# One set of buffer pools through the whole kernel, and output stages that take all first block products before the second ones

## The chip, the cores and the metric

The kernel runs on one core of one Trainium2 chip. A core has a matrix engine (TensorE, PE in the profile; its weight loads are PEld), a vector engine (VectorE, DVE), an activation engine (ScalarE, ACT), a general engine (GpSimd, POOL), a queue engine (SyncE, SP) and 16 DMA engines. Each engine runs its own instruction stream in order. Memory on the chip is SBUF (working tiles, 128 partitions) and PSUM (eight banks, which TensorE writes). The metric is the device time of one execution in microseconds (us).

## What is computed

A decoder block on `x` (1024 tokens by 1024 channels), all in float32:

```python
h = rms_norm(x, norm_g)
z = h @ w_in                      # 1024 x 9216: q_r k_r v_r gate_r q_d k_d v_d gate_d mg_r mg_d
o_r = rms_norm(retention(q_r, k_r, v_r)) * silu(gate_r)      # branch 0
o_d = rms_norm(diff_attention(q_d, k_d, v_d)) * silu(gate_d) # branch 1
m = sigmoid(mg_r) * (o_r @ ret_w_o) + sigmoid(mg_d) * (o_d @ diff_w_o)
out = x + m @ w_out
```

## The kernel before

A float32 operand of a matrix product is cut into a high and a low part (`split`, `cut`: ScalarE rounds the high part, VectorE subtracts it), and a product takes three matmuls: high by high, high by low, low by high.

**Mixer part.** Two retention groups (`rqk`, `rv`) and eight attention heads (`d0` to `d7`) project their columns of `w_in` with the normalised, transposed input `hT`. Weight tiles come from the pool `wpool` (tag `w`, `NWS` = 11 buffers; raw loads with tag `wraw`, 3 buffers). The small pieces of each token block are put on a clock of ticks (`after`, `among`) and dealt out between the projection's matmuls. The pool `dp` holds the attention heads' tiles.

**Output part.** The gates' columns of `w_in` (16 pairs of 128-wide strips, numbered `q`), the two branch projections (`y0`, `y1`) and the final projection (`out`) are products of a 2 by 2 block matrix with a 2 by 2 block matrix, done in Winograd's form with seven block products. A block product is 12 matmuls of 128x512 (`product`: four chunks of the contraction, three matmuls each). The right-hand side is `r11`, `r21`, `r22` and the combinations `t1` to `t4`, each in one home tile (`HOME`), so a stage's `t2` can only be written when the stage before has read its own for the last time. `early_r` loads and cuts `r11` and `r21`; `late_r` loads the blocks, forms the sums on VectorE and cuts them (for the gates it takes them from `hT`). Loads and sums pass through staging tiles with tag `rs` (6 buffers). The left-hand side of a pair: the first two block products (`firsts`; the bank is called `X`, with operands `la`) give the block c(0,0) and a partial result `p1`; the other five are in `Pair.one` (banks `y`, `w`, `z`, against `t2`, `t3`, `t1`) and `Pair.two` (`w` against `t4`, `z` against `r22`). `rest_ops` loads a pair's strips (`ra`, `rb`; tag `raw`, 3 buffers), forms four sums on VectorE (tag `sf`, 4 buffers) and cuts five operands (tag `l`, 8 buffers). `rests` interleaves `two` of one pair with `one` of the next, and prepares the pair after.

**Which tiles meet.** `first_duo(q)` computes the first two block products of two gate pairs in the mixer part, for q = 0 to 10; `first[q]` in DRAM keeps them. Pairs 12 to 15 are done at the start of the output part by `firsts("hm", ...)`. Between the two parts `mixers.close()` gives up `wpool`, `gp` (result tiles `ft`, tag `gt`) and the PSUM pool `ps`; the output part opens `act2`, `lp`, `fp` and a PSUM pool `pb` of eight banks over the same memory and over that of `dp`.

**Merging the branches.** Each branch block is multiplied by its gate (`sg`, loaded into tag `ld`, 2 buffers) and goes to `md` in DRAM: branch 0 by a plain store from SP, branch 1 by a DMA from GpSimd that adds to what is there (line 919). The final projection reads its left-hand side from `md`; the rows of `md[0]` come from branch pairs 0 and 1, those of `md[1]` from pairs 2 and 3.

**Order.** The program is traced in the order of the code, and a planner (`schedule_with_timeline_sim`) turns it into one static instruction stream for each engine, from a model of times and with program order as priority. A tile with a tag gets a buffer when an earlier tile of that tag is released.

## Time and profile before

| | |
|---|---|
| median of three runs | 1324.86 us (1323.21 to 1325.03) |
| profiled execution | 1322.55 us, of which 1320.8 us span |
| TensorE | busy 1264.3 us, 96% of the span |
| VectorE | busy 950.9 us, 72% |
| ScalarE | busy 651.4 us, 49% |
| GpSimd | busy 265.4 us, 20% |
| mixer part, without its last drain | up to 792 us |
| gate pairs | about 800 to 1065 us |
| branch projections | about 1062 to 1228 us |
| final projection | about 1218 us to the end |

TensorE is busy nearly throughout, so time is lost where it stands still or where its granted clock is below full speed. The shares of the other engines are averages over parts that differ much, and are read by stretch.

### The profile page before, as it was taken

To read this page: it belongs to the slowest core of one execution; us is meant where nothing else is said; L and a number is where in the kernel's file an instruction comes from. 1 tells how busy PE (TensorE), PEld (TensorE's weight loads), DVE (VectorE), ACT (ScalarE), POOL (GpSimd) and SP (SyncE) were. 2 spreads that over 40 slices of the span, in tenths; PEclk is the share of its full clock that TensorE was granted. 3 is DMA by queue.
4 is the path that set the end of the run, shared out by engine and by line. 5 is a ranking of instruction groups with operands and counts; after the bars stand their busy time and mean duration, and the time that the engine had idled before them with its cause. 6 is when DMAs were issued, how large, how long until landed. Compare 5 with 4: busy or idle time off the path is not lost.

```text
span 1320.8 us, 19793 instructions
## 1 busy us (share of the span) xinstructions
PE 1264.3 (96%) x6836; PEld 1113.4 (84%) x6836; DVE 950.9 (72%) x2016; ACT 651.4 (49%) x1448; POOL 265.4 (20%) x371
## 2 busy tenths in 40 slices
PE   7999999999999999999999997899989999998698
PEld 5888888889999999999999885687778888876586
DVE  7436435737786877777687838987876699998884
ACT  6235123527575766767676724434454454442420
POOL 3134113323333534243333100000000000012000
PEclk9999999999999999999999998899999999999799
DMA  7202120431010101102020326578876578998963
GB/s 259 66 29 72 57 72 8 125 107 49 9 57 9 57 10 56 55 11 65 9 72 9 120 89 201 189 256 276 298 251 208 160 245 274 301 277 178 253 191 112
DMA packets 157750, 169.95 MB, mean 129 GB/s; under 512 B 9921, under 2 KB 108369, under 8 KB 157649
## 3 DMA queue, kind: packets, MB, share of 16 engines
q1 hardware_dynamic: 154816, 163.68, 38.4%
q0 software_dynamic: 2832, 5.00, 2.6%
q8 instruction: 54, 0.88, 0.3%
q14 instruction: 48, 0.39, 0.1%
HBM read 122.51 MB, written 46.14 MB: 128 GB/s over the span
## 4 chain that ended last, share of the span: by engine, by line
PE 67%; DVE 13%; DMA 11%; issue 4%; ACT 3%; POOL 2%; SPq 1%; DVEq 0%; ACTq 0%; POOLq 0%
PE z_d L121 18%; PE z_rv L121 7%; PE z_rqk L121 6%; PE fb L130 5%; PE sps L533 5%; PE dops L573 5%; PE z_h L130 3%; PE w_h L130 3%; PE aT L560 2%; DMA og<-c_h 2%; PE X_out L130 2%; PE z_out L130 2%; PE w_out L130 2%; PE y_h L130 1%; DMA r_o<-og 1%
## 5 line engine op out<-in xcount | busy, mean ns | idle before, releaser
L121 PE MATMUL z_d<-w_d,hT 128*128 128x384 f32 x1536 | 303.5, 340 | 1.4 <-DVE nsq L488 1.4
L121 PEld LDWEIGHTS z_d<-w_d,hT 128*128 128x128 f32 x1536 | 264.3, 188 | 4.5 <-ACT V L479 1.7
L539 ACT ACTIVATE S<-S,ast 128x256 f32<-128x256 f32 (+7 forms) x128 | 99.0, 774 | 33.4 <-DVE ast L535 32.0
L533 PE MATMUL sps<-K,Q 128*128 128x512 f32 (+5 forms) x384 | 107.5, 363 | 0.5 <-ACT Q L516 0.5
L919 POOL DMA_DIRECT2D md<-c_y x16 | 13.9, 869 | 435.0 <-DVE ls_y L663 372.7
L121 PE MATMUL z_rv<-w_rv,hT 128*128 128x512 f32 x384 | 98.8, 397 | 0.0
L121 PE MATMUL z_rqk<-w_rqk,hT 128*128 128x512 f32 x384 | 94.1, 398 | 0.9 <-ACT hT L283 0.9
L121 PEld LDWEIGHTS z_rqk<-w_rqk,hT 128*128 128x128 f32 x384 | 70.9, 190 | 15.8 <-ACT hT L283 1.6
L573 PE MATMUL dops<-V,aTs 128*128 128x128 f32 x576 | 78.7, 275 | 0.0
L121 PEld LDWEIGHTS z_rv<-w_rv,hT 128*128 128x128 f32 x384 | 68.7, 188 | 11.8
L573 PEld LDWEIGHTS dops<-V,aTs 128*128 128x128 f32 x576 | 76.6, 191 | 2.2 <-ACT aTs L562 0.2
L535 DVE CUSTOM_DVE_ANT_0 S<-sps,ndist 128x512 f32<-128x512 f32 (+5 forms) x128 | 67.9, 533 | 10.4 <-PE sps L533 10.1
L130 PE MATMUL fb<-hT,fw 128*128 128x512 f32 x288 | 71.5, 396 | 0.0
L91 POOL TENSOR_TENSOR nss<-ms_n,mh 128x4 f32<-128x4 f32 x64 | 67.2, 1051 | 4.3
L533 PEld LDWEIGHTS sps<-K,Q 128*128 128x128 f32 x384 | 63.2, 189 | 3.1 <-ACT Q L516 1.5
L130 PEld LDWEIGHTS fb<-hT,fw 128*128 128x128 f32 x288 | 52.7, 188 | 10.2
L490 POOL TENSOR_TENSOR nsq<-nsq,gh 128x256 f32<-128x256 f32 x64 | 47.5, 746 | 63.7 <-DVE nsq L488 62.4
L550 DVE SCALAR_TENSOR_TENSOR S<-S,ast,S 128x128 f32<-128x128 f32 (+3 forms) x64 | 55.5, 868 | 1.2
L130 PE MATMUL z_h<-hT,ls_h 128*128 128x512 f32 x192 | 48.4, 401 | 6.0 <-DVE c_h L810 5.9
L130 PE MATMUL y_h<-t_h,ls_h 128*128 128x512 f32 x192 | 49.0, 398 | 3.3 <-ACT t_h L662 3.3
L662 ACT ACTIVATE ls_h<-s_h 128x512 fp32r<-128x512 f32 x64 | 38.6, 621 | 27.0 <-PE z_h L130 18.6
L130 PE MATMUL w_h<-t_h,l_h 128*128 128x512 f32 x192 | 48.4, 398 | 3.5 <-DVE u_h L822 3.5
(251 smaller groups left out, 2760.3 us busy)
## 6 DMA issues: line engine op xcount, KB each, us to landing
wr_d<-in_w_in_dram SPq DMA_DIRECT2D x96, 128.0 KB, 2.8
ra_h<-in_w_in_dram SPq DMA_DIRECT2D x16, 512.0 KB, 4.2
rb_h<-in_w_in_dram SPq DMA_DIRECT2D x16, 512.0 KB, 5.3
s<-sg SPq DMA_DIRECT2D x32, 256.0 KB, 4.2
fr<-in_w_in_dram SPq DMA_DIRECT2D x12, 512.0 KB, 4.8
first<-ft SPq DMA_DIRECT2D x24, 256.0 KB, 2.0
og<-c_h SPq DMA_DIRECT2D x24, 256.0 KB, 4.4
sg<-c_h SPq DMA_DIRECT2D x24, 256.0 KB, 3.3
```

The lines of the kernel that those rows point to most:

```text
L91: nc.gpsimd.tensor_tensor(out_t, ms, mh[:, :n], ALU.pow)
L121: nc.tensor.matmul(o, a[k][:, i0, asl], b[k][:, i1, bsl], start=(k == 0 and j == 0), stop=(k == NK - 1 and j == 2))
L130: nc.tensor.matmul(bank, L[:, i0, j * P:(j + 1) * P], R[:, j, i1, :], start=(start and j == 0 and i == 0), stop=(j == 3 and i == 2), skip_ ...
L490: nc.gpsimd.tensor_tensor(sq, sq, hd["g"], ALU.mult)
L533: nc.tensor.matmul(sp[:, :m], hd["Q"][t][:, j, e, :], hd["K"][:, j, c], start=(e == 0), stop=(e == 1))
L535: nc.vector.tensor_tensor_reduce(sb[:, c], sp[:, :m], ndist[:, S - n + m * f:S - n + m * f + m], -slope, FMAX if f == 0 else st[:, j:j + 1 ...
L539: nc.scalar.activation(sb[:, :n], sb[:, :n], AF.Exp, bias=st[:, j:j + 1], scale=-1.0, accum_out=st[:, 2 + j:3 + j])
L550: nc.vector.scalar_tensor_tensor(S0[:, :n], S1[:, :n], st[:, 6:7], S0[:, :n], ALU.mult, ALU.add)
L560: nc.tensor.transpose(tp[:, b * P:(b + 1) * P], A[:, c:c + P], ident)
L573: nc.tensor.matmul(o[:, :P], aT[:, b, :], hd["V"][f][:, b, :], start=(kb == 0), stop=(kb == t))
L662: nc.scalar.activation(dst_hi, src, AF.Copy)
L919: nc.gpsimd.dma_start(m, t, accum_op=ALU.add)
```

## The change

`wpool`, `gp` and `ps` stay open to the end (`mixers` is gone) with `NWS` = 10. The output part uses their tiles: cut operands take tag `w` (10 buffers, before `l` with 8), raw strips tag `wraw` (3, as `raw` had), results tag `gt` (3, as `c` had), and the eight banks are the tags `pj`, `s`, `tr`, `o` of `ps` in a fixed turn. The four sums of `rest_ops` have lost their own tag and share `rs`, which now has 7 buffers for both. Pairs 12 to 15 go through `first_duo` as the others do, behind `late_r("h", None)` in the code; the weights of pairs 12 and 13 are asked for in `first_duo(10)`. `firsts` takes the first block product of all four pairs, then the second of all four. The last pair of branch 1 (p = 3, four blocks) loads its part of `md`, adds on VectorE and stores it from SP.

```diff
-NWS = 11
+NWS = 10
...
-    mixers = ExitStack()
-    wpool = mixers.enter_context(tc.tile_pool(name="wpool", bufs=NWS))
-    ps = mixers.enter_context(tc.tile_pool(name="ps", bufs=2, space=bass.MemoryType.PSUM))
+    wpool = ctx.enter_context(tc.tile_pool(name="wpool", bufs=NWS))
+    gp = ctx.enter_context(tc.tile_pool(name="gp", bufs=3))
+    ps = ctx.enter_context(tc.tile_pool(name="ps", bufs=2, space=bass.MemoryType.PSUM))
...
         for q in range(4, 12, 2):
-            first_duo(q, (lambda q=q: more(q + 2, q + 3)) if q < 10 else (lambda: None))
+            first_duo(q, lambda q=q: more(q + 2, q + 3))
         drain()
-    mixers.close()
...
-    pb = ctx.enter_context(tc.tile_pool(name="pb", bufs=8, space=bass.MemoryType.PSUM))
...
     def stage(name):
-        return lpool.tile([P, 512], F32, tag="rs", name=name, bufs=6)
+        return lpool.tile([P, 512], F32, tag="rs", name=name, bufs=7)
...
     def left(name, src):
-        L = lpool.tile([P, 2, 512], F32R, tag="l", name=name, bufs=8)
+        L = wpool.tile([P, 2, 512], F32R, tag="w", name=name)
...
     def raw_l(name):
-        return lpool.tile([P, 4, 2, P], F32, tag="raw", name=name, bufs=3)
+        r = wpool.tile([P, 2, 512], F32, tag="wraw", name=name, bufs=3)
+        return r.rearrange("p a (b n) -> p (a b) n", n=P).rearrange("p (j s) n -> p j s n", s=2)
...
     def rest_ops(name, src):
...
-        s1, s2, s3, s4 = (lpool.tile([P, 4, P], F32, tag="sf", name=f"s{i}_{name}", bufs=4)
+        s1, s2, s3, s4 = (stage(f"s{i}_{name}").rearrange("p (j n) -> p j n", n=P)
                           for i in range(1, 5))
...
+    turn = [0]
+
     def bank(name):
-        return pb.tile([P, 512], F32, tag="b", name=name)
+        tag, n = (("pj", NPJ), ("s", NS), ("tr", NTR), ("tr", NTR),
+                  ("pj", NPJ), ("s", NS), ("tr", NTR), ("o", 1))[turn[0] % 8]
+        turn[0] += 1
+        return pst(tag, name, n)
...
     def firsts(name, srcs, done):
...
+        ops = [load(0, i) for i in range(2)]
+        for kh in range(2):
+            for i in range(n):
+                k = kh * n + i + 2
+                if k < 2 * n:
+                    ops.append(load(k // n, k % n))
+                run(product(X[i], ops[kh * n + i], RB["r21" if kh else "r11"], kh == 0))
+                if kh == 0:
+                    p1.append(temp("p1", f"p1_{name}{i}", 4))
+                    nc.scalar.activation(p1[i], X[i], AF.Copy)
+                else:
+                    done(i, X[i])
         return p1
...
-    p1 = firsts("hm", [hsrc(q) for q in range(12, 16)], keep(12))
     late_r("h", None)
-    for i, t in enumerate(p1):
-        nc.sync.dma_start(first[12 + i][:, 0, :], t)
-    rests([gate_pair(q) for q in range(16)])
+    first_duo(12, lambda: more(14, 15))
+    pairs = [gate_pair(q) for q in range(16)]
+    first_duo(14, pairs[0].prep)
+    rests(pairs, True)
...
                 m = rows(md[i // 4][:, i % 4], half)
-                if br == 0:
+                if p == 3 and br == 1:
+                    o = temp("ld", f"m{i}{half}", 2)
+                    nc.sync.dma_start(o, m)
+                    nc.vector.tensor_tensor(t, t, o, ALU.add)
+                if br == 0 or p == 3:
                     nc.sync.dma_start(m, t)
                 else:
                     nc.gpsimd.dma_start(m, t, accum_op=ALU.add)
```

## Rows read from the trace of the kernel before

**Rows 1.** The page: busy time, share of span and instructions of each engine.

```profile
PE 1264.3 (96%) x6836; PEld 1113.4 (84%) x6836; DVE 950.9 (72%) x2016; ACT 651.4 (49%) x1448; POOL 265.4 (20%) x371
```

**Rows 2.** Stretches: length, then busy us (instructions) by engine, clock, DMA share, GB/s.

```profile
300.00:740.00 440.00, 438.83 (x2906) 426.49 (x2905) 334.48 (x975) 307.67 (x821) 161.96 (x237) 1.00 0.14 40
760.00:792.00 32.00, 32.00 (x172) 27.27 (x170) 10.04 (x21) 8.55 (x16) 2.25 (x3) 1.00 0.24 90
792.00:860.00 68.00, 52.87 (x203) 41.30 (x202) 61.41 (x102) 27.41 (x48) 0.00 (x0) 0.87 0.61 192
860.00:1060.00 200.00, 192.80 (x838) 157.81 (x837) 151.59 (x242) 88.26 (x145) 0.00 (x0) 0.99 0.73 241
1060.00:1165.00 105.00, 105.00 (x465) 86.91 (x465) 101.45 (x170) 50.04 (x88) 2.17 (x3) 1.00 0.84 274
1206.00:1240.00 34.00, 18.92 (x76) 14.90 (x75) 24.25 (x40) 10.12 (x18) 6.05 (x7) 0.82 0.96 232
1240.00:1250.00 10.00, 9.99 (x35) 7.55 (x34) 10.00 (x18) 6.11 (x11) 0.00 (x0) 0.77 1.08 339
```

**Rows 3.** Timeline of TensorE between the two parts: start us, us, instructions, idle before.

```profile
789.34 2.99 PE L130 MATMUL fb<-hT,fw 128*128 128x512 f32 x12
800.34 1.22 PE L130 MATMUL X_hm<-hT,la_hm 128*128 128x512 f32 x2 [8.02 <-ACT la_hm L662]
803.05 3.35 PE L130 MATMUL X_hm<-hT,la_hm 128*128 128x512 f32 x7 [1.48 <-ACT la_hm L662]
```

**Rows 4.** The chain that ended last, between the two parts: start us, us, what.

```profile
790.34 2.27 DMA ot_d<-doT
...
793.16 3.19 DMA first<-ft
...
797.39 4.96 DMA ra_hm<-in_w_in_dram
```

**Rows 5.** Timeline of ScalarE and GpSimd where `dp` opens over a closed pool.

```profile
286.15 0.39 ACT L478 ACTIVATE nsq<-z_d 128x256 f32<-128x256 f32 x1 [6.03 <-DMA ot_r<-roTs]
...
286.30 0.29 POOL L469 COPY gh<-gains 128x128 f32<-128x128 f32 x1 [9.62 <-DMA ot_r<-roTs]
```

**Rows 6.** Timeline of VectorE: the first instruction of `late_r("h", None)`.

```profile
796.62 0.69 DVE L670 TENSOR_TENSOR r11s_h<-hT 128x512 f32<-128x512 f32 x1 [3.51 <-DMA o<-ot_r]
```

**Rows 7.** Timeline of TensorE between branch 1 and the final projection.

```profile
1217.87 1.22 PE L130 MATMUL X_out<-r_w,la_out 128*128 128x512 f32 x2 [3.42 <-ACT la_out L662]
1218.89 3.79 PE L130 MATMUL w_y<-t_o,l_y 128*128 128x512 f32 x12
1222.52 2.43 PE L130 MATMUL X_out<-r_w,la_out 128*128 128x512 f32 x10
1224.79 2.88 PE L130 MATMUL z_y<-r_o,ls_y 128*128 128x512 f32 x12
1239.34 2.88 PE L130 MATMUL X_out<-r_w,la_out 128*128 128x512 f32 x5 [11.66 <-ACT la_out L662]
```

**Rows 8.** The chain that ended last, into that second stop of TensorE.

```profile
1227.46 6.86 DMA md<-c_y
...
1234.38 4.20 DMA ra_out<-md
...
1238.65 0.64 ACT la_out L662
```

**Rows 9.** DMA issues: queue, count, size, median us from issue to landing.

```profile
s<-sg SPq DMA_DIRECT2D x32, 256.0 KB, 4.2
...
md<-c_y SPq DMA_DIRECT2D x16, 256.0 KB, 3.7
md<-c_y POOLq DMA_DIRECT2D x16, 256.0 KB, 5.7
```

**Rows 10.** Timeline of SP: last strip load of the gates, first of branch 0.

```profile
1015.54 0.38 SPq L762 DMA_DIRECT2D rb_h<-in_w_in_dram  x1
...
1027.04 2.12 SPq L753 DMA_DIRECT2D ra_y<-in_ret_w_o_dram  x4
```

More of the change, by code (lines that the diff above doesn't have):

```diff
@@ L248, in proj @@
         return z
-    gp = mixers.enter_context(tc.tile_pool(name="gp", bufs=3))
     with tc.tile_pool(name="rq", bufs=8) as rq, ExitStack() as early:
@@ L744, in raw_l @@
     def raw_l(name):
-        return lpool.tile([P, 4, 2, P], F32, tag="raw", name=name, bufs=3)
-    def first_ops(name, src):
-        L = []
-        for kh in range(2):
-            if kh == 0:
-                r = raw_l(f"ra_{name}")
-            nc.sync.dma_start(r[:, :, kh:kh + 1, :], src(kh, 0, 1))
-        for kh in range(2):
-            L.append(left(f"la{kh}_{name}", r[:, :, kh, :]))
-        return L
+        r = wpool.tile([P, 2, 512], F32, tag="wraw", name=name, bufs=3)
+        return r.rearrange("p a (b n) -> p (a b) n", n=P).rearrange("p (j s) n -> p j s n", s=2)
     def rest_ops(name, src):
@@ L773, in rest_ops, with load @@
         return A, [left(f"l22_{name}", l22), left(f"ls4_{name}", s4)]
+    turn = [0]
     def bank(name):
-        return pb.tile([P, 512], F32, tag="b", name=name)
+        tag, n = (("pj", NPJ), ("s", NS), ("tr", NTR), ("tr", NTR),
+                  ("pj", NPJ), ("s", NS), ("tr", NTR), ("o", 1))[turn[0] % 8]
+        turn[0] += 1
+        return pst(tag, name, n)
     def temp(tag, name, bufs=None):
+        if tag == "c":
+            return gp.tile([P, 512], F32, tag="gt", name=name, bufs=3)
         return fp.tile([P, 512], F32, tag=tag, name=name, **(dict(bufs=bufs) if bufs else {}))
     def firsts(name, srcs, done):
-        ops = [first_ops(f"{name}{i}", s) for i, s in enumerate(srcs[:2])]
-        X, p1 = [], []
-        for i in range(len(srcs)):
-            X.append(bank(f"X_{name}{i}"))
-            run(product(X[i], ops[i][0], RB["r11"], True))
-            p1.append(temp("p1", f"p1_{name}{i}", 4))
-            nc.scalar.activation(p1[i], X[i], AF.Copy)
-            if i > 0:
-                run(product(X[i - 1], ops[i - 1][1], RB["r21"], False))
-                done(i - 1, X[i - 1])
-                if i + 1 < len(srcs):
-                    ops.append(first_ops(f"{name}{i + 1}", srcs[i + 1]))
-        run(product(X[-1], ops[-1][1], RB["r21"], False))
-        done(len(srcs) - 1, X[-1])
+        n = len(srcs)
+        X = [bank(f"X_{name}{i}") for i in range(n)]
+        p1 = []
+        def load(kh, i):
+            r = wpool.tile([P, 2, 512], F32, tag="wraw", name=f"rf_{name}{kh}{i}", bufs=3)
+            r = r[:, 0, :].rearrange("p (j n) -> p j n", n=P)
+            nc.sync.dma_start(r.unsqueeze(2), srcs[i](kh, 0, 1))
+            return left(f"la{kh}_{name}{i}", r)
+        ops = [load(0, i) for i in range(2)]
[10 more added lines that the diff above has]
+                    done(i, X[i])
         return p1
@@ L831, in two, with rests @@
             self.c(0, 1, self.z, self.u2, ALU.subtract)
-    def rests(pairs):
-        pairs[0].prep()
+    def rests(pairs, ready=False):
+        if not ready:
+            pairs[0].prep()
         before = iter(())
@@ L854, in hsrc @@
         return strips(w_in, pair_col[q])
-    def keep(q):
-        def done(i, b):
-            t = temp("c", f"c11_{q + i}")
-            nc.vector.tensor_copy(t, b)
-            nc.sync.dma_start(first[q + i][:, 1, :], t)
-        return done
     def gate_pair(q):
```

## Prediction, made before the changed kernel was run

> **What bounds the kernel now.** I read the page's engine line first, then stretches, then the timelines and the chain of waits at the places where TensorE stops. TensorE is busy 96% of the span [rows 1], so the question is where the rest goes. By stretches [rows 2]: the attention heads lose nearly nothing (438.83 of 440 us busy at full clock); the branch projections lose nothing either, and there 465 matmuls take 105 us, 0.226 us each. I use that as the price of a matmul at full clock (2.4 GHz). Two places stand out. From 792 to 860 us, 203 matmuls would need 45.8 us and take 68: 22 us lost. From 1206 to 1250 us, 76 + 35 = 111 matmuls would need 25.1 us and take 44: 19 us lost. The 200 us between (838 matmuls, 189 us) lose 11, in waits of the gate pairs on VectorE that this change does not address.
>
> *Between the two parts.* TensorE's last mixer matmul ends at 792.3, the first of the output part starts at 800.3, and it stops again until 803.05 [rows 3]. The chain [rows 4] is: last attention store landed at 792.6, then a store of `ft` at 796.4, then a strip load of 5 us. The output part's pools wait for that store. A pool waits as a whole for all that lay below it: where `dp` opened, ScalarE and GpSimd were let go at 286.15 and 286.30, into two tiles, by one and the same store [rows 5]. Behind the stop, TensorE is not alone in being late. VectorE starts `late_r` at 796.62 [rows 6] and is busy 61.4 of the 68 us to 860, with 102 instructions at 0.602 us each [rows 2]: it sets the pace there, and is idle before (10 of 32 us busy up to 792).
>
> *Before the final projection.* TensorE waits 3.42 us, does one first product and the last two products of branch 1, and waits 11.66 us [rows 7]. The wait is for a second block product's operand: GpSimd's accumulating DMA takes 6.86 us to land, SP's load of the result 4.20, the cut 0.64 [rows 8]. The clock is at 0.82 and 0.77 around it [rows 2].
>
> **The change part by part.**
>
> *Pools kept, pairs 12 to 15 by `first_duo`.* The operands of pairs 12 and 13 no longer wait for any pool: their cuts, and very likely those of 14 and 15, fit into the idle VectorE before 792 [rows 2]. TensorE can go straight on with the same 96 matmuls (21.7 us, to 814). But the products behind them need `t2`, `t3`, `t1` from `late_r`, whose staging pool now lies over `dp` and so opens when `dp`'s last store has landed, at 792.6 instead of 796.4 [rows 4 to 6]: 3.8 us sooner. On VectorE the eight `la` cuts of pairs 12 to 15 leave the crowded stretch: 8 x 0.602 = 4.8 us. The copies of the results stay (four `keep`, now four `ft`). As VectorE sets the pace, I take what it gains: 3.8 + 4.8 = **8.6 us**. Bounds: below, 0, if `late_r`, which stands ahead of `first_duo(12)` in the code, makes the copies wait that free the two `pj` banks for pairs 14 and 15; above, all 22 us. I take the middle value, since the row of VectorE's count is the one that says what TensorE waits for.
>
> *All first products, then all second.* Three more first products (36 matmuls, 8.1 us) can run while the second operand is on its way; so far they ran after the 11.66 us stop. A stop of 3 to 4 us remains. The clock stays up too: 35 matmuls in 10 us where full clock makes 44 [rows 2], 2.1 us. Together 10.2 us. In `y0` and `y1` TensorE did not stop at this place, so nothing is gained.
>
> *Plain merge of the last pair.* Instead of 6.86 us for the accumulating DMA: an add (0.6) and a store from SP, 3.7 us by the median against 5.7 [rows 9]; 2 to 2.6 us sooner. But each block now needs two `ld` tiles of two, and a load into one takes 4.2 us [rows 9]: up to 4.2 us later. I let these cancel: the operand comes when it came before. Four adds on VectorE cost 4 x 0.6 = 2.4 us if it is full; I charge them. The Trainium skill's "DMA: Bandwidth & Descriptors" (Issuing engines are not separate DMA queues) says that a transfer moved to another issuing engine saves only the time of its issue. By that the merge would bring next to nothing; the rows here show 2 us between the two kinds, though the accumulating one also reads. The sum hangs on neither.
>
> So the second place gives 10.2 - 2.4 = **7.8 us**; bounds 3 (VectorE, 24 of 34 us busy there, has no more than 10 to give, and its cuts wait for the same loads) and 15 (the 11.66 and 3.42 us stops gone).
>
> *Sums share `rs`.* This is the part that can cost. Within a tag, buffers go out in program order: weights of branch 0 that wait for nothing but a `raw` buffer were loaded at 1027.0, right behind the gates' last strip at 1015.5 [rows 10]. So far `early_r` and `late_r` of the next stage could fill six `rs` buffers and work ahead while the sums used their own four. Now the 44 tiles of a stage (28 and 16) go through seven: the next stage's 8 cuts and first 6 sums (14 x 0.602 = 8.4 us of VectorE) move behind the last pair's sums, and the first pair's sums behind `late_r`'s last loads. VectorE is 101 of 105 us busy there [rows 2]. Bounds per stage: 0 (the ten `w` buffers let the sums run further ahead than eight `l` did, and the work-ahead is only shifted) and 8.4. Nearest is VectorE's idle share, 3.5 of 105 us, which cannot take it all. I charge 2 us each for `y1` and `out`, 1 for `y0`: **5 us**.
>
> *The rest at nothing.* Ten `w` buffers instead of eleven in the mixers: the next head's third tile rather than the fourth waits for the last token block; TensorE's 440 us at full clock are the cover. If it went, one cut per switch (0.64 + 0.60 us) at eleven switches is 14 us. The turn of the banks: eight as before. Halved strip loads in `firsts`: same bytes.
>
> Sum: 8.6 + 7.8 - 5 = 11.4 us off the profiled execution's 1322.55, 1311. The median of the runs lies 2.3 us above that execution: 1313.5, **1313** as forecast.
>
> **The rivals.**
>
> *Both holes close* (chance 0.17). If VectorE's work in the first place is only needed in part before TensorE goes on (36 instructions of `late_r`, 4 copies, 3 for the first operand: 43 x 0.602 = 25.9, to 818.5, against TensorE's 814), 22 us of loss shrink to 6, and the second gives 13. With no price for `rs`: 29 us, 1296. For it: VectorE's order before mixed in work for later pairs. Against: the later pairs need it soon after.
>
> *The holes close but VectorE takes it back* (0.12): what TensorE gains it waits for later, as VectorE has 3.5 us left in 105. The first place gives 3.8, the second 3, `rs` costs 5: 1323, no change. The same comes out if the planner, which sorts by its own times, orders `firsts` much as before.
>
> *Shared staging makes it slower* (0.17). At each of the three entries into `y0`, `y1` and `out`, the 8.4 us of work that used to be done ahead arrive with TensorE waiting. 3 x 8.4 = 25 against 16.4 gained: 1333. It decides from 5.5 us a stage. For it: VectorE 101 of 105 us busy. Against: gates leave VectorE idle (151.6 of 200) before `y0`, and `w` grew by two. The Trainium skill's "Perfetto Trace Analysis" (Optimization Strategy) warns that the same gap repeated on the engine that should be full can mean too few buffers for the next tile; that is this mechanism. The trace of before has no such gap at these entries [rows 2]: TensorE is full from 1060 to 1165.
>
> *The mixers pay for the tenth buffer* (0.04): 14 us against 11.4, 1327. Against it stands a TensorE that idles 1.2 us in 440.
>
> **How the numbers follow.** The forecast's own case (0.50) spans 1305 to 1320. A difference under 0.2%, 2.6 us, can't be told from none. Faster takes the forecast and the first rival, and a little of the second: 0.69. Same is most of the second: 0.12. Slower is the staging, the mixers and a rest of the second: 0.19. The range leaves out the lower half of the first rival and the upper half of the third: 1298 to 1330.
>
> **What would show it.** Right: TensorE runs through 792 to 814 without a stop and then stops for `t` operands, with VectorE full; VectorE starts `late_r` near 792.6; before the final projection 48 first-product matmuls run together and the stop behind them is 3 to 4 us; `y1` shows new short stops of TensorE on VectorE. Wrong: `late_r` starting well before 792 (pools open tile by tile), a stop in `first_duo(14)` behind `pj`, staging loads that come far later than before with stops of over 6 us at `y0` or `y1`, or any idle TensorE at the switches between heads.

## The result and the profile after

The changed kernel takes 1326.69 us (median of 20 runs), the kernel before 1324.24 beside it: ratio 1.0023, 95% interval 1.0012 to 1.0033. It is slower, by about 2.5 us, where 1313 and "faster" were forecast. (Single executions of one kernel spread by some 8 us here, so times are compared by medians. A profile is one execution, with a span of 1324.2 us for the changed kernel, and what is read from it carries that spread.) The page's engine line, against [rows 1]:

```profile
PE 1260.6 (95%) x6836; PEld 1112.0 (84%) x6836; DVE 954.6 (72%) x2020; ACT 647.4 (49%) x1448; POOL 265.3 (20%) x367
```

The same stretches as in [rows 2]:

```profile
300.00:740.00 440.00, 438.81 (x2914) 428.28 (x2913) 339.17 (x979) 305.39 (x822) 164.08 (x237) 1.00 0.14 41
760.00:792.00 32.00, 32.00 (x169) 27.33 (x168) 15.90 (x30) 12.39 (x24) 2.74 (x3) 1.00 0.47 152
792.00:860.00 68.00, 52.91 (x221) 42.53 (x220) 64.92 (x108) 29.13 (x49) 0.00 (x0) 0.87 0.58 187
860.00:1060.00 200.00, 187.27 (x809) 151.94 (x808) 138.72 (x222) 81.23 (x135) 0.00 (x0) 0.99 0.69 223
1060.00:1165.00 105.00, 102.61 (x449) 83.51 (x448) 98.60 (x164) 47.37 (x83) 0.00 (x0) 1.00 0.81 265
1206.00:1240.00 34.00, 31.14 (x138) 25.46 (x136) 28.91 (x48) 14.13 (x24) 3.96 (x5) 1.00 0.89 247
1240.00:1250.00 10.00, 0.00 (x0) 0.00 (x0) 9.45 (x17) 3.52 (x7) 0.00 (x0) 0.50 0.94 316
```

The heads are unchanged. From 792 to 860 TensorE does 18 matmuls more than before, but in the gate stage (860 to 1060) 29 fewer, and VectorE is *less* busy there than before, 138.7 against 151.6: it waits. At the end, 62 matmuls more up to 1240, then none for 10 us. Both old holes are still there, elsewhere. TensorE's timeline at the first place, then VectorE's in the same stretch:

```profile
790.85 22.18 PE L130 MATMUL fb<-hT,fw 128*128 128x512 f32 x96
828.10 1.22 PE L130 MATMUL y_h<-t_h,ls_h 128*128 128x512 f32 x2 [15.07 <-ACT ls_h L658]
```
```profile
794.21 0.69 DVE L666 TENSOR_TENSOR r11s_h<-hT 128x512 f32<-128x512 f32 x1 [2.82 <-DMA ot_d<-doT]
...
821.89 0.68 DVE L659 TENSOR_TENSOR t_h<-r22s_h,t_h 128x512 fp32r<-128x512 f32 x1
...
824.30 0.68 DVE L666 TENSOR_TENSOR s_h<-ra_h,rb_h 128x512 f32<-128x512 f32 x1
...
826.71 0.67 DVE L666 TENSOR_TENSOR s_h<-s_h,ra_h 128x512 f32<-128x512 f32 x1
```

The 96 first products run without a stop, 13.8 us ahead of before (they end at 813.0, before at 826.8). Then TensorE waits 15.1 us, not for a `t` operand (`t2` is cut at 821.9) but for `ls_h`, the first pair's own operand: its sums come at 824.3 and 826.7, late in VectorE's row, although their strips were asked for at 773.8 and 781.5 and landed within 4 us. With this one stop the lead is gone: the first gate product starts at 828.1, before at 826.7. Before the out stage, TensorE's timeline (against [rows 7]) and the chain of waits (against [rows 8]):

```profile
1222.02 2.88 PE L130 MATMUL w_y<-t_o,l_y 128*128 128x512 f32 x12
1224.73 3.79 PE L130 MATMUL X_out<-r_w,la_out 128*128 128x512 f32 x16
1228.36 2.88 PE L130 MATMUL z_y<-r_o,ls_y 128*128 128x512 f32 x12
1231.08 6.05 PE L130 MATMUL X_out<-r_w,la_out 128*128 128x512 f32 x26
1251.41 1.83 PE L130 MATMUL X_out<-r_w,la_out 128*128 128x512 f32 x3 [14.28 <-ACT la_out L658]
```
```profile
1241.78 0.70 DVE c_y L914
1242.49 4.66 DMA md<-c_y
1247.23 3.48 DMA rf_out<-md
1250.73 0.64 ACT la_out L658
```

The 48 first products run without a stop, but the operand comes 26.5 us after the last `w_y` product (1224.9 to 1251.4); before it was 16.6 (1222.7 to 1239.3, [rows 7]).

To place gains and losses, four points of TensorE's timeline serve as marks in every kernel (start of the group plus its length): A, end of the last gate product; B, end of the last `w_y` product, from which the out stage's last operand is made; C, restart of the second products of the out stage; D, end of the last matmul.

| kernel | A | B | C | D | A to B | B to C | C to D | median (before, run beside it) |
|---|---|---|---|---|---|---|---|---|
| before | 1067.0 | 1222.7 | 1239.3 | 1315.8 | 155.7 | 16.6 | 76.5 | 1324.2 |
| changed | 1070.1 | 1224.9 | 1251.4 | 1319.8 | 154.8 | 26.5 | 68.4 | 1326.7 (1324.2) |
| e1_accum | 1072.3 | 1229.5 | 1252.9 | 1322.7 | 157.2 | 23.4 | 69.8 | 1328.9 (1322.9) |
| e2_mring | 1070.0 | 1223.5 | 1244.4 | 1312.6 | 153.5 | 20.9 | 68.2 | 1319.9 (1322.9) |
| e3_t4last | 1072.2 | 1225.5 | 1251.9 | 1319.9 | 153.3 | 26.4 | 68.0 | 1324.9 (1322.9) |
| e4_sums | 1056.2 | 1225.7 | 1249.3 | 1321.2 | 169.5 | 23.6 | 71.9 | 1333.8 (1322.9) |
| f_order | 1068.6 | 1224.6 | 1245.8 | 1317.1 | 156.0 | 21.2 | 71.3 | 1321.9 (1322.4) |
| f_merge | 1067.5 | 1219.7 | 1243.8 | 1319.3 | 152.2 | 24.1 | 75.5 | 1327.3 (1322.4) |
| f_order_merge | 1066.7 | 1225.3 | 1246.2 | 1314.5 | 158.6 | 20.9 | 68.3 | 1321.4 (1323.4) |
| f_pools | 1072.5 | 1223.3 | 1243.0 | 1319.3 | 150.8 | 19.7 | 76.3 | 1331.0 (1322.4) |
| f_best | 1065.8 | 1223.9 | 1248.0 | 1316.0 | 158.1 | 24.1 | 68.0 | 1323.5 (1322.4) |
| x_mixed | 1061.8 | 1222.5 | 1245.0 | 1314.0 | 160.7 | 22.5 | 69.0 | 1318.7 (1322.8) |
| v_before | 1065.7 | 1215.9 | 1237.2 | 1313.2 | 150.2 | 21.3 | 76.0 | 1319.0 (1322.8) |
| v_mring | 1069.8 | 1232.5 | 1254.4 | 1324.4 | 162.7 | 21.9 | 70.0 | 1328.2 (1322.8) |
| v_mixed | 1056.4 | 1220.4 | 1241.5 | 1309.7 | 164.0 | 21.1 | 68.2 | 1315.8 (1322.8) |
| s_mixed3 | 1050.9 | 1209.8 | 1234.2 | 1302.2 | 158.9 | 24.4 | 68.0 | 1309.2 (1322.7) |
| s_noadd3 | 1067.0 | 1226.4 | 1249.9 | 1319.6 | 159.4 | 23.5 | 69.7 | 1326.7 (1322.7) |
| g_before | 1067.5 | 1227.9 | 1251.6 | 1328.2 | 160.4 | 23.7 | 76.6 | 1334.8 (1323.4) |
| g_after | 1069.7 | 1240.9 | 1261.9 | 1331.1 | 171.2 | 21.0 | 69.2 | 1338.1 (1323.4) |
| g_best | 1063.0 | 1231.1 | 1248.8 | 1323.5 | 168.1 | 17.7 | 74.7 | 1330.0 (1323.4) |

Each row is one execution. How far one can be off shows at A: the six kernels with the gate stage of before (before, f_order, f_merge, f_order_merge, g_before, v_before) lie between 1065.7 and 1068.6, the six with that of the changed kernel (changed, e1_accum, e2_mring, f_pools, g_after, v_mring) between 1069.7 and 1072.5. So a difference of less than 3 us between two rows is not told from noise. The rows of e4_sums and f_pools are of their fastest execution, 5 us under the median.

Changed against before: +3.1 us up to A, -0.9 in the output stages, +9.9 of waiting for the operand, -8.1 behind it. Sum +4.0, as D shows. The 0.9 is within the noise; the 3.1 counts, since the two groups do not overlap at A.

### The profile page after: what moved, and what is told of

Its sections match the earlier page's. It is cut to its first block, busy times and chain, and to the rows that moved or that the text cites. A ratio compares the mean times of both kernels' runs of the same rounds, so it can differ in the third digit from the quotient of the medians.

```text
span 1324.2 us, 19831 instructions
## 1 busy us (share of the span) xinstructions
PE 1260.6 (95%) x6836; PEld 1112.0 (84%) x6836; DVE 954.6 (72%) x2020; ACT 647.4 (49%) x1448; POOL 265.3 (20%) x367
## 5 line engine op out<-in xcount | busy, mean ns | idle before, releaser
L918 POOL DMA_DIRECT2D md<-c_y x12 | 10.5, 872 | 433.4 <-DVE c_y L909 422.3
L130 PE MATMUL fb<-hT,fw 128*128 128x512 f32 x384 | 94.3, 396 | 0.9 <-ACT ft L229 0.9
L130 PEld LDWEIGHTS fb<-hT,fw 128*128 128x128 f32 x384 | 70.3, 188 | 14.9 <-ACT ft L229 1.1
L571 PE MATMUL dops<-V,aTs 128*128 128x128 f32 x576 | 81.8, 276 | 0.0
L121 PEld LDWEIGHTS z_rv<-w_rv,hT 128*128 128x128 f32 x384 | 68.7, 188 | 11.7
L488 POOL TENSOR_TENSOR nsq<-nsq,gh 128x256 f32<-128x256 f32 x64 | 50.2, 788 | 73.4 <-DVE nsq L486 62.0
L130 PE MATMUL y_h<-t_h,ls_h 128*128 128x512 f32 x192 | 48.6, 401 | 15.1 <-ACT ls_h L658 15.1
L130 PEld LDWEIGHTS y_h<-t_h,ls_h 128*128 128x128 f32 x192 | 37.1, 194 | 23.9 <-ACT ls_h L658 15.5
L130 PEld LDWEIGHTS w_h<-t_h,l_h 128*128 128x128 f32 x192 | 36.3, 192 | 20.8 <-DVE u_h L823 12.1
```

The lines of the kernel that those rows point to most:

```text
L121: nc.tensor.matmul(o, a[k][:, i0, asl], b[k][:, i1, bsl], start=(k == 0 and j == 0), stop=(k == NK - 1 and j == 2))
L130: nc.tensor.matmul(bank, L[:, i0, j * P:(j + 1) * P], R[:, j, i1, :], start=(start and j == 0 and i == 0), stop=(j == 3 and i == 2), skip_ ...
L488: nc.gpsimd.tensor_tensor(sq, sq, hd["g"], ALU.mult)
L571: nc.tensor.matmul(o[:, :P], aT[:, b, :], hd["V"][f][:, b, :], start=(kb == 0), stop=(kb == t))
```

## The experiments

### The merge: whose delay is it?

**e1_accum**: the accumulating DMA is back for the last pair, all else as changed.

```diff
-                if p == 3 and br == 1:
-                    o = temp("ld", f"m{i}{half}", 2)
...
-                if br == 0 or p == 3:
+                if br == 0:
```

> The changed kernel with one part undone: the last pair of the second output stage adds its block to the store in DRAM by the accumulating DMA again, as in the kernel before. The changed kernel took 1326.7 us (median), the kernel before 1324.2. Theory A: the plain merge is what kept the reordered first products from paying; its two staging buffers make the loads and the adds wait for each other, and the first operand of the out stage comes about 10 us later than before. With the accumulating DMA the stop of TensorE behind the 48 first products (14.3 us in the changed kernel) falls to 4 to 6 us and the time to 1316 to 1319. Rival B: a block is merged no sooner by the accumulating DMA, since GpSimd's queue and the read-modify-write take what the ring takes now: the stop stays at 12 to 14 us and the time at 1325 to 1328.

1328.9 us, ratio 1.0049 (1.0035 to 1.0062): theory A is missed. The stop is still 12.3 us, as rival B said, and B comes 4.6 us later. Without the merge the kernel is not faster but slower than the changed one (1.0049 against 1.0023, 3.4 us): even through the ring of two, the merge is not what kept the change from paying.

**e2_mring**: the merge stays, three of its four loads get buffers that are free by then.

```diff
-                    o = temp("ld", f"m{i}{half}", 2)
+                    o = temp(*(("p1", f"m{i}{half}", 4) if strip or half else ("ld", f"m{i}{half}", 2)))
```

> The changed kernel with the plain merge kept, but three of its four loads of the first branch's block go into buffers of the p1 ring, free by then, so that they no longer share the ring of two with the loads of the gate's values. Theory A (the ring of two is the delay): the loads stand ready when the product comes, the operand of the out stage comes as early as with the accumulating DMA or up to 2 us earlier, the stop falls to 3 to 6 us, the time to 1315 to 1319. Rival B (the merge is slow because VectorE is late with the products and the plain store takes as long as the other): the stop stays at 11 to 14 us, 1324 to 1327.

1319.9 us, 0.9978 (0.9964 to 0.9993): faster than both. B to C falls from 26.5 to 20.9 us. In the chain of this kernel the last add starts 5.9 us earlier (1.4 of them at B), and the store lands in 2.65 us instead of 4.66:

```profile
1235.87 0.61 DVE c_y L914
1236.50 2.65 DMA md<-c_y
1239.22 4.47 DMA rf_out<-md
1243.72 0.64 ACT la_out L658
```

So the merge does pay for its ring of two, as theory A said; but 7.8 us of the stop remain, not 3 to 6. Against e1_accum, with the accumulating DMA, it is 9.1 us faster, of which the marks put only 2.5 between B and C.

**f_merge**: the merge alone, on the kernel before, through the ring of two.

```diff
+                if p == 3 and br == 1:
+                    o = temp("ld", f"m{i}{half}", 2)
+                    nc.sync.dma_start(o, m)
+                    nc.vector.tensor_tensor(t, t, o, ALU.add)
+                if br == 0 or p == 3:
-                if br == 0:
```

> The kernel before with the plain merge of the last pair alone, through its two staging buffers. Theory A (loads and adds wait for each other in the ring of two): the out stage's operand comes 3 to 8 us later, 1327 to 1332. Rival H (the merge is slow only together with the new order and the shared ring, which fill VectorE and the queues there): the store is 2 to 3 us faster, the time 1321 to 1325.

1327.3 us, 1.0037 (1.0025 to 1.0050). B to C grows by 7.5 us, 3.0 of them because B comes earlier; the operand itself (C) comes 4.5 us later. On the kernel before, theory A holds and rival H falls.

### The order of the first products

**f_order**: the new loop for the two output stages and the out stage, on the kernel before (its own rings, its accumulating DMA).

```diff
+    def firsts_turned(name, srcs, done):
...
-        p1 = firsts(f"y{br}", srcs, first_y)
+        p1 = firsts_turned(f"y{br}", srcs, first_y)
...
-    p1 = firsts("out", [m_src(i) for i in range(4)], first_out)
+    p1 = firsts_turned("out", [m_src(i) for i in range(4)], first_out)
```

> The kernel before with one part of the change alone: the two output stages and the out stage take all first block products, then all second ones; pools, rings and the accumulating DMA are those of before. Theory A (as predicted): the last operands come when they came, 36 matmuls fill the hole before the out stage and the time falls by 8 to 10 us, to 1313 to 1316. Theory F: the order brings VectorE's and the queue's work for the out stage forward into the stretch of the last pair, so the last operand comes 3 to 6 us later and only 3 to 6 us are gained: 1318 to 1321. Rival G: what the out stage gains, the two output stages lose by banks and buffers held longer: 1322 to 1326.

1321.9 us, 1.0000 (0.9989 to 1.0010): no difference. The number is next to rival G's 1322, the mechanism is nearer theory F's: A to B is 0.3 us longer, C to D shrinks by 5.2, B to C grows by 4.6. VectorE's timeline in this kernel, behind the last `w_y` product (it ends at 1224.6):

```profile
1224.43 1.28 DVE L663 TENSOR_TENSOR t_w<-r11s_w,t_w 128x512 fp32r<-128x512 f32 x2
1225.64 0.69 DVE L663 TENSOR_TENSOR la_out<-rf_out,la_out 128x512 fp32r<-128x512 f32 x1
...
1229.84 0.68 DVE L835 TENSOR_TENSOR c_y<-w_y,u_y 128x512 f32<-128x512 f32 x1
...
1231.05 0.68 DVE L663 TENSOR_TENSOR la_out<-rf_out,la_out 128x512 fp32r<-128x512 f32 x1
...
1232.85 0.68 DVE L939 TENSOR_TENSOR c_y<-c_y,s 128x512 f32<-128x512 f32 x1
```

VectorE does not stop between the product's end and its eviction, but takes it up 5.3 us after the end; in the kernel before, the same eviction stands at 1224.68, 2.0 us after. In between stand one of the `la_out` cuts that the new order wants early, two `t_w` cuts, two evictions and two gate products of other blocks, and two sums. That the new order put them there is argued from this row, not tested alone; it fits that what fills the hole also lengthens it.

**f_order_merge**: f_order with the merge and its own buffers.

```diff
+                    o = temp(*(("p1", f"m{i}{half}", 4) if strip or half else ("ld", f"m{i}{half}", 2)))
...
+                if br == 0 or p == 3:
-                if br == 0:
```

> The kernel before with the new order of the first products and the plain merge, its loads in buffers of the p1 ring; pools, rings and gate stage are those of before. The order alone made no difference, the merge through the ring of two alone cost 5 us. Theory A (the ring of two is what the merge pays for): together 1316 to 1320, as the changed kernel with these buffers (1319.9). Rival K (that gain needs the pools of the change as well): 1321 to 1325.

1321.4 us, 0.9986 (0.9973 to 0.9998). B to C is 20.9 with the plain merge and 21.2 with the accumulating DMA: with buffers of its own the merge is neutral there. The time lies in rival K's range, above theory A's: order and merge with these buffers gain 1.9 us on the pools of before, and 11.6 on those of the change (f_pools, below, to e2_mring). What they are worth depends on the pools and rings that they stand on.

### The first place and the gate stage

**f_pools**: the rest of the change alone (old order, accumulating DMA).

```diff
     def firsts(name, srcs, done):
-        n = len(srcs)
...
+        ops = [first_ops(f"{name}{i}", s) for i, s in enumerate(srcs[:2])]
```

> The changed kernel without the new order of the first products (these are taken as in the kernel before) and with the accumulating DMA: what is left of the change is the pools kept through the kernel, the ring of seven that sums and staging share, ten left-operand buffers, and the first products of pairs 12 to 15 in the earlier form. Theory A (the shared ring loses the lead by pair 15 of the gate stage and costs the output stages 2 us each): 1325 to 1330, and no lead over the kernel before at the end of the gate stage. Rival (the prediction's terms, 8.6 us gained and 5 us lost): 1319 to 1322.

1331.0 us, 1.0066 (1.0051 to 1.0082): theory A, 1 us above its range. At A it is 5.5 us behind the kernel before, after 14 us of lead at 813.

With this run four kernels form a chain, each one step from the next: f_pools 1.0066, with the new order 1.0049 (e1_accum), with the merge 1.0023 (the changed kernel), with the merge's own buffers 0.9978 (e2_mring). In time that is 8.7 us slower, then 2.2, 3.4 and 6.0 faster. So taken first, the part with the pools and rings, which was forecast to gain 3.6 us, is the one that loses. Taken last, from f_order_merge (0.9986) to e2_mring, it gains 1.1. Either way it does not bring what was forecast; how the loss divides among the parts hangs on the order in which they are taken.

**e3_t4last**: the `t4` sums behind the first pair's own.

```diff
+    def late_t4(name, src):
...
     first_duo(14, pairs[0].prep)
+    late_t4("h", None)
```

> The changed kernel with the four t4 sums of the gate's right operand taken out of the block that comes before the first products of pairs 12 to 15, and put behind the first gate pair's own sums; nothing else differs. Theory A: the stop of 15.1 us of TensorE behind these products is the first pair's sums waiting, in the shared ring, for buffers behind the t4 sums; moved ahead, the first pair starts some 4 to 7 us sooner, VectorE being full in this stretch. Since the lead is gone by pair 15 of the gate stage all the same, the time is 1324 to 1327. Rival C: what is lost at the start of the gate stage is lost to the end: the time falls with the stop, to 1319 to 1322. Rival D: the stretch is VectorE's own work alone, in whatever order: the stop stays at 13 to 15 us.

1324.9 us, 1.0017 (1.0003 to 1.0030). TensorE's timeline:

```profile
820.22 1.22 PE L130 MATMUL y_h<-t_h,ls_h 128*128 128x512 f32 x2 [7.41 <-ACT ls_h L658]
```

The first pair starts at 820.2 instead of 828.1, so rival D falls: about half of the first stop is the sums' place behind the `t4` sums. At A nothing of it is left (1072.2), as theory A expected; so in this kernel something takes it back further on, and the ring is the suspect.

**e4_sums**: the ring of seven parted, 4 for sums and 3 for staging.

```diff
-        return lpool.tile([P, 512], F32, tag="rs", name=name, bufs=7)
+        return lpool.tile([P, 512], F32, tag="rs", name=name, bufs=3)
...
-        s1, s2, s3, s4 = (stage(f"s{i}_{name}").rearrange("p (j n) -> p j n", n=P)
+        s1, s2, s3, s4 = (sfp.tile([P, 4, P], F32, tag="sf", name=f"s{i}_{name}", bufs=4)
```

> The changed kernel with the shared ring of seven parted again within the same memory: four buffers for the sums of a pair, three for the staging of the right operands (six and four in the kernel before). Theory A (the shared ring): pair 0's sums no longer wait for staging buffers, the stop of 15.1 us falls to 5 to 9 us, and the later gate pairs keep the lead: 1318 to 1322, although three staging buffers cost 1 to 2 us at each output stage. Rival E (in the later gate pairs it is the ten left-operand buffers, against eight before, that put VectorE's work for later pairs ahead of the evictions): the first stop falls as well, the lead is still gone by pair 15, 1325 to 1329.

1333.8 us, 1.0084 (1.0066 to 1.0101), slower than either theory said, and yet its trace settles their dispute: there is no stop of 15 us, and A comes 13.9 us *earlier* than in the changed kernel, with the same ten left-operand buffers. So rival E falls, and the shared ring is what loses the lead up to A. Then A to B takes 169.5 us; with the same gate stage and all seven buffers behind it (x_mixed, below) it takes 160.7. It fits that three staging buffers are too few there, but x_mixed also has the merge's own buffers, and its A comes later.

**f_best**: rings of 4 and 5, nine left-operand buffers, the merge's own buffers.

```diff
-NWS = 10
+NWS = 9
...
-        return lpool.tile([P, 512], F32, tag="rs", name=name, bufs=7)
+        return lpool.tile([P, 512], F32, tag="rs", name=name, bufs=5)
```

> The changed kernel with sums and staging in rings of their own (four and five buffers, paid for by a ninth instead of a tenth left-operand buffer), and the merge's loads in buffers of the p1 ring. Theory A: the 7 us that the parted ring gained at the start of the gate stage stay, the 6 us of the merge's own buffers add up with them, and five staging buffers instead of three keep the output stages from losing: 1308 to 1315. Rival I (the ninth buffer costs the mixers 3 to 6 us, five staging buffers cost the output stages another 3): 1317 to 1323.

1323.5 us, 1.0006 (0.9993 to 1.0019): near rival I. A gains only 4.2 us on e2_mring, A to B loses 4.6.

**x_mixed**: parted (4 and 3) in the gate stage alone, all seven for both afterwards, and the merge's own buffers.

```diff
+    def ring(name, own):
+        if not gate[0]:
+            own = count[0] % 7 >= 3
+            count[0] += 1
+        return lpool.tile([P, 512], F32, tag="sf" if own else "rs", name=name, bufs=4 if own else 3)
```

> The changed kernel with the merge's own buffers, and with sums and staging parted (four and three buffers) in the gate stage alone; from the first output stage on all seven go out to sums and staging alike, as in the changed kernel. Theory V (what is ahead at 1060 us is taken back in the two output stages, where VectorE has no time left): the kernel is some 9 us ahead of the one without the parted rings at 1060 us, and ends within 3 us of it: 1317 to 1321. Rival (a lead of the gate stage lives on, and the earlier parted kernels lost it to their three or five staging buffers): 1308 to 1313.

1318.7 us, 0.9970 (0.9959 to 0.9982). Against e2_mring, from which it differs in the rings alone, it is 8.2 us ahead at A and 1.0 at B, as theory V said. Where the lead is made, the stretch to 860 us of e2_mring and of x_mixed shows:

```profile
792.00:860.00 68.00, 52.90 (x220) 42.57 (x220) 65.15 (x108) 29.00 (x49) 0.00 (x0) 0.87 0.59 189
```
```profile
792.00:860.00 68.00, 62.47 (x251) 48.21 (x249) 64.89 (x108) 28.97 (x49) 0.00 (x0) 0.95 0.56 178
```

The stop of 15.1 us is gone, and 31 matmuls (7.0 us) more are done by 860; from there to 1060 it is 808 against 809. So the parting pays at the first stop, and the gate pairs behind it keep what it gave. The ring can be seen at work in those pairs too. VectorE's timeline in the changed kernel, then TensorE's:

```profile
986.29 0.69 DVE L666 TENSOR_TENSOR s_h<-ra_h,rb_h 128x512 f32<-128x512 f32 x1 [3.99 <-issue]
...
988.23 0.68 DVE L823 TENSOR_TENSOR u_h<-w_h,u_h 128x512 f32<-128x512 f32 x1
```
```profile
988.96 3.06 PE L130 MATMUL w_h<-t_h,l_h 128*128 128x512 f32 x12 [0.86 <-DVE u_h L823]
```

Waits of VectorE and TensorE from 860 to 1060 us, first of the changed kernel, then of this one (us, times, longest):

```profile
DVE l_h L659 <- ACT l_h L658: 15.3, 9, 3.5
...
DVE s_h L666 <- issue: 9.9, 3, 4.0
...
PE w_h L130 <- DVE u_h L823: 9.1, 7, 2.4
```
```profile
DVE s_h L666 <- DMA rb_h<-in_w_in_dram: 16.0, 7, 3.8
...
DVE l_h L659 <- ACT l_h L658: 6.1, 4, 2.1
DVE c_h L878 <- DMA o<-ot_r: 3.8, 3, 2.2
...
DVE c_h L878 <- DMA o<-ot_d: 2.8, 6, 0.9
...
PE w_h L130 <- DVE u_h L831: 3.9, 2, 3.2
```

The sums' waits for nothing that the profile names (9.9 us) are gone, those of the `l_h` cuts fall by 9.2. It fits that a sum without a buffer holds the eviction `u_h` behind it in VectorE's order, and TensorE with it; what the sum waits for the profile does not name. Other waits of VectorE grow in their place (`r11s_o` for its load, 7.1 us), and all of TensorE's waits on VectorE there fall only from 11.7 us in e2_mring (12.7 in the changed kernel) to 9.9.

### Why the lead does not reach the end

**g_before, g_after, g_best**: 36 of VectorE's adds given to GpSimd, on three kernels.

```diff
-            add(r11, r11, r12)
+            sums = nc.gpsimd if src else nc.vector
+            sums.tensor_tensor(r11, r11, r12, ALU.add)
...
```

> The kernel before with 36 of VectorE's adds (the twelve sums r11, r12, r22 of the right operand in each of the three later stages) given to GpSimd, which is nearly idle there; an add takes VectorE 0.60 us and GpSimd about 1.04 by the rows of the kernel before. Theory V: from 1060 us on VectorE is the engine that sets the end (in the kernel before it is busy 140.7 of the 146 us from 1060 to 1206, and its backlog delays the last pair's products): the hole before the out stage shrinks by 2 to 5 us, but TensorE has hardly a stop before it, so no more is gained: 1317 to 1321. Rival (TensorE sets the two output stages, transfers the hole): 1321 to 1324. Rival: GpSimd's slower adds come late and hold the accumulating DMAs behind them on its queue: 1325 to 1330.

> The changed kernel with the same 36 adds given to GpSimd. Theory V: VectorE's backlog from 1060 us on is what eats the lead and delays the merge; with 7 us less of it in each stage the stop of 14.3 us falls to 6 to 10 us and the time to 1314 to 1320. Rival J (the ring of two alone makes the stop): the stop stays at 12 to 14 us, 1323 to 1327.

> The kernel of the last call with parted rings of four and five, nine left-operand buffers and the merge's own buffers (it was some 7 us ahead at 1060 us and lost all of it by 1240), with the 36 adds given to GpSimd. Theory V: the lead it had at the end of the gate stage now lives on to the end: 1306 to 1314, against 1323.5 without. Rival (the lead is lost to something else than VectorE: nine buffers, banks or transfers): 1318 to 1323.

1334.8 us (1.0085, 1.0072 to 1.0098), 1338.1 (1.0103, 1.0089 to 1.0118) and 1330.0 (1.0036, 1.0022 to 1.0051). All are slower than any expectation, and no test of theory V, since VectorE was not relieved: see the last section.

**v_before, v_mring, v_mixed**: the same 36 adds left out, loads and cuts kept. What these kernels compute lacks the sums, so only their times are of use.

```diff
-            add(r11, r11, r12)
+            if not src:
+                add(r11, r11, r12)
...
```

> The kernel before without the twelve sums r11, r12, r22 of the right operand in each of the three later stages (the loads stay, the operands are cut from the plain blocks): 36 adds, 21.7 us of VectorE's time at 0.60 us each, are left out. Theory V (VectorE sets these stages): TensorE has few stops to lose before 1206 us, the hole before the out stage shrinks: 1312 to 1317. Rival (the holes are transfers' time): 1320 to 1324.

> The changed kernel with the merge's own buffers (1319.9 before), without the same 36 adds. Theory V: the stop before the out stage (7.8 us) and the stops in the two output stages close: 1306 to 1312. Rival (transfers): 1317 to 1320.

> The first kernel of this call without the 36 adds. Theory V: with VectorE's time given back, the lead of the gate stage lives on: 6 to 9 us faster than the third kernel of this call, 1298 to 1305, while with the adds the two differ by at most 3 us. Rival: the two differ by the same with the adds and without.

1319.0 us (0.9965, 0.9950 to 0.9981), 1328.2 (1.0040, 1.0028 to 1.0052) and 1315.8 (0.9951, 0.9937 to 0.9964). The first lies between its two expectations. v_mixed is 12.5 us faster than v_mring, while with the adds the two differ by 1.2: that much theory V had said, though both times lie above all that was expected. But v_mring is 8.4 us *slower* than e2_mring, which does 21.7 us more work on VectorE. If VectorE's work as such set the end, less of it could not do that. With the adds gone, VectorE stands in waits instead (30 us idle from 1060 to 1245 us, against 11 in e2_mring); in v_mring:

```profile
DVE c_y L910 <- DMA s<-sg: 8.0, 5, 3.6
DVE t_o L659 <- ACT t_o L658: 5.2, 2, 2.7
DVE t_o L666 <- DMA t_o<-og: 4.6, 2, 3.4
```

**s_mixed3, s_noadd3**: a third buffer in the ring `ld`, one `u3` buffer less, on x_mixed and on v_mring.

```diff
-            self.u3 = temp("u3", f"u3_{n}", 2)
+            self.u3 = temp("u3", f"u3_{n}", 1)
...
-                o = temp("ld", f"o{br}{h}{half}", 2)
+                o = temp("ld", f"o{br}{h}{half}", 3)
...
-                s = temp("ld", f"s{br}{i}{half}", 2)
+                s = temp("ld", f"s{br}{i}{half}", 3)
```

> The kernel with parted rings in the gate stage alone and the merge's own buffers (1318.7, the fastest that does all the work), with three instead of two buffers in the ring through which the gate's values are loaded, paid for by one u3 buffer instead of two. Theory S (in the two output stages the loads of the gate's values, issued only when a buffer of the ring of two comes free, hold VectorE's queue): VectorE waited 2.6 us for them before 1245 us; 1314 to 1317. Rival (these waits only stand in for others): 1317 to 1321.

> The kernel with the merge's own buffers and without the 36 adds (1328.2, slower than with them), with the same ring of three. Theory S: of its loss the 8.0 us that VectorE waited for the gate's values go: 1314 to 1321. Rival (the order in VectorE's queue, of which these waits are only one form): 1324 to 1330.

s_noadd3: 1326.7 us, 1.0032 (1.0019 to 1.0046): the rival; the ring is not what v_mring lost. s_mixed3: **1309.2 us, 0.9898 (0.9882 to 0.9914)**, 13.5 us under the kernel before, the fastest of all, and better than either expectation. The place was not the one expected: 10.9 us come before A, in the gate stage, where the same ring carries the attention's outputs `o`. From 860 to 1060 us TensorE does 45 matmuls more than in x_mixed. The two waits for `o` in the list of x_mixed above (6.6 us, nine times) are gone from this kernel's, TensorE's waits on VectorE fall from 9.9 to 4.7 us, and its last gate product ends at 1050.9. (That A can also fall at 1056.4 with a ring of two, in v_mixed, leaves open how much of the 10.9 is the third buffer's; the medians differ by 9.5.) And 13.7 of the 19.1 us that it leads e2_mring by at A are still there at B, with all of VectorE's work in place. Theory V as a rule ("what is ahead is taken back") falls with that.

## Why the prediction was wrong

The forecast took 11.4 us off, the result adds 2.5. By the chain above, the part with the pools and the shared ring has 12.3 of these 14 us: a gain of 8.6 less 5 was forecast, and f_pools shows a loss of 8.7. For the order and the merge 7.8 were forecast, and from f_pools to the changed kernel they bring 5.7. The chain is one way to divide a total whose parts do not add up; A, which neither order nor merge touches, is firmer: there the kernels with the change are 3 us late instead of 8.6 early.

**Pools kept (8.6 us).** Right: the staging pool waits for `dp`'s last store, which none of the waiting instruction's operands needs (VectorE starts at 794.21 on it, 2.4 us sooner than before where 3.8 were forecast); TensorE runs without a stop to 813; VectorE is full behind it. Wrong: what TensorE stops for, and that the gain lasts. With the ring parted the gain is there: x_mixed is 5.2 us ahead of the kernel before at A (1061.8 against 1067.0).

**Sums share `rs` (5 us, at the entries of `y0`, `y1`, `out`).** This is the step that failed first. The rule it used, buffers in program order, fits what was seen, and it named "the first pair's sums behind `late_r`'s last loads"; but it was priced only where the next stage works ahead, and at nothing at the entry into the gate stage. There the first pair's sums waited behind `late_r`'s, and TensorE 15.1 us for them. Up to A it costs 8.2 us (e2_mring against x_mixed) to 13.9 (changed against e4_sums). At the entries, where 5 us were charged, A to B is 0.9 us shorter than before. How much of the loss at A reaches the end is another matter: x_mixed ends only 1.2 us before e2_mring.

**All first, then all second (10.2 us).** The cover was sized well in the changed kernel: C to D is 8.1 us shorter, 36 matmuls. The 2.1 us of clock did not come: it is 0.50 from 1240 to 1250, where TensorE stands still. Wrong was "a stop of 3 to 4 us remains"; it is 14.3. That took the operand's arrival as fixed; alone, the order lengthens B to C by 4.6 us and shortens C to D by 5.2, which leaves nothing that can be measured. On the pools of the change it is worth 2.2 us (f_pools to e1_accum).

**Plain merge ("I let these cancel").** The ring of two was mis-sized here. Its price was put at up to 4.2 us and set against a gain of 2 to 2.6; with buffers of its own the changed kernel is 6.0 us faster (0.9978 against 1.0023). Against the accumulating DMA the merge through that ring costs 4.9 us on the kernel before (f_merge) and gains 3.4 on the changed one (e1_accum), so no one number holds for it. With its own buffers it does cancel from B to C on the kernel before (20.9 against 21.2 us) and on the changed one the two are 2.5 us apart (20.9 against 23.4), little for one pair of traces; the 2.4 us charged for its adds are too small to be seen apart. The Trainium skill's "DMA: Bandwidth & Descriptors" (Issuing engines are not separate DMA queues), by which the other queue brings next to nothing, is tested by no run here: in these pairs the kind of transfer and VectorE's adds change along with the queue.

**At nothing.** The tenth `w` buffer costs the mixers nothing: 438.81 of 440 us, as before.

**The rivals.** "Shared staging makes it slower" named the right resource and the wrong place; its test, stops over 6 us at `y0` or `y1`, shows 1.6 us at most (in `y1`). The right test would have been the gate stage, which the prediction set aside as not touched by the change. That the measured time lies inside the stated range is owed to this rival, which held its upper end, and is no support for the forecast's own account. That too few buffers show as stops of the engine that should be full was the Trainium skill's warning there ("Perfetto Trace Analysis", Optimization Strategy); the trace agrees: TensorE's repeated stop for `u_h` (9.1 us, seven times) falls to 3.9, twice, with the parted ring.

**Open.** In x_mixed and s_mixed3 the stretch A to B is 5 to 7 us longer than in e2_mring, and 9 longer in v_mring. Each time VectorE's queue waits somewhere else; what sets this stretch I cannot say, and so not what decides how much of a lead at A reaches the end. Why the order and the merge are worth more on the pools of the change than on those of before is not shown either. Whether a third `ld` buffer alone helps the kernel before was not tried. In s_mixed3 the `u3` ring changed with it. The fixed turn of the banks and the ten left-operand buffers of the output part were not undone by themselves.

## What to carry to other kernels

When two uses are put on one ring, price the sharing in every stage that draws on it, its first use included, and ask which tile stands in front of which: on an engine that runs its stream in order, a tile without a buffer is a stop for all behind it. A hole that waits for an operand is not a fixed size: work moved into it, or loads added on the way to it, go through the same queues that make the operand. Mark a few points of the bottleneck's timeline in every variant; a lead that is made and lost again can't be seen in the totals. And undo the parts of a change one after the other as well as one at a time: here they do not add up.

## What the hardware showed

GpSimd's adds did not relieve VectorE. In g_before, GpSimd's adds and VectorE's instructions from 1050 us on (groups by line: count, busy us, mean ns), then VectorE's of the kernel before:

```profile
L702 POOL TENSOR_TENSOR r11s_w<-r11s_w,r12s_w 128x512 f32<-128x512 f32 x4 | 6.7, 1679 | 13.4 <-DMA r12s_w<-in_w_out_dram 13.4
```
```profile
L663 DVE TENSOR_TENSOR ls_y<-s_y,ls_y 128x512 fp32r<-128x512 f32 x32 | 26.5, 828 | 0.0
...
L811 DVE TENSOR_TENSOR c_y<-z_y,u_y 128x512 f32<-128x512 f32 x16 | 10.8, 681 | 2.6 <-DMA md<-c_y 2.0 <-PE z_y L130 0.6
```
```profile
L663 DVE TENSOR_TENSOR ls_y<-s_y,ls_y 128x512 fp32r<-128x512 f32 x32 | 21.5, 681 | 0.0
```

The 32 cuts `ls_y` of g_before once more, as shortest, median and longest (ns):

```profile
L663 DVE TENSOR_TENSOR ls_y<-s_y,ls_y x32: 671/680/1775, 1077.9 to 1212.7; 128x512 fp32r<-128x512 f32 x32
```

An add takes GpSimd 1.45 to 1.71 us by group, where the expectation had 1.04 from its work in the attention part. VectorE's subtractions of two SBUF tiles grow from 681 to 828 ns in the mean, while those with one operand in PSUM (`z_y`) stay at 681. The mean hides two kinds: six of the 32 take 1177 to 1775 ns, all of them beside an add of GpSimd, the others 671 to 687. VectorE's total is 951.4 us with 36 adds fewer, 950.9 before. The Trainium skill's "SBUF — State Buffer" (Who interferes with whom) states this: a VectorE instruction with two SBUF inputs contends with a GpSimd instruction that reads SBUF, one with at most one such input does not. The trace agrees on both halves.
